# Convolution and pooling projections behind all gates, the weight split behind a step's events, and another form of the norm's scale

## The chip, the cores and the metric

The kernel runs on one core of a Trainium2 chip. The metric is the device time of one execution in microseconds. The kernel before took 1755.76 us, the median of three runs (1753.92 to 1758.45).

## The reference

The reference is one inference step of a two-layer network on 128 context tokens and 256 latent tokens, which share all weights. Each layer is a feed-forward block, a token mixer and another feed-forward block, each followed by a layer norm and modulated by a condition vector:

```
h = x * (1 + mod[3i+1]) + mod[3i]                         # modulate(i)
x = layer_norm(ALPHA*x + 0.5*mod[2]*swiglu(modulate(0)))
z = h @ w_in + b_in                                       # mixer, h = modulate(1)
q, k, v, cg, pu, gt = split(z)
att  = diff_attention(q, k, v) -> rms_norm -> @ w_att_o
conv = silu(layer_norm(depthwise_conv(a * sigmoid(g)))) @ w_conv_o     # 31 taps
pool = multiscale_pool(pu) @ w_pool_o
ga, gc, gp = split(sigmoid(gt))
x = layer_norm(ALPHA*x + mod[5] * ((ga*att + gc*conv + gp*pool) @ w_out + b_out))
x = layer_norm(ALPHA*x + 0.5*mod[8]*swiglu(modulate(2)))
```

All tensors are float32. The mod vectors are `silu(cond) @ w_mod`, 144 column blocks of 128, computed while the rest runs.

## The kernel before

All 384 tokens go through every matmul together, features on the partitions. A weight unit is a 128x1024 block of weights, and there is a fixed list of them (`_unit_specs`), in the order in which TensorE uses them. Each fp32 product is made of three fp32r matmuls (`mm3`, L402): the weights are split into a high part `wh`, cast by ScalarE (L342), and a low part `wl`, subtracted by VectorE (L351). So a unit is 24 matmuls of 384 columns. It has five buffer pairs (`NW`), and in some stretches (`extra`) up to four more, made of six of the 66 general slots of 128x384.

All instructions are written in an order fixed by hand. `begin(key)` (L372) opens a unit, a step: it prepares the units up to `lead` ahead (DMA, cast, split), then runs the events that are due at this step (`at(n, fn)`, `run_events`), then the folds (`run_after`), then `bg_rate` items of the background queue `bg`, then VectorE's modulation work, of which `mod_rate` jobs per unit are due. Each engine takes its instructions in that order. In the output projection of the mixer (`early`) the events run ahead of the preparation. `lead` starts at two behind a norm and rises by one per unit to five plus `extra`.

A mixer opens with units for the convolution's input (multiplied inside the norm), then q and k (steps 1 to 6), v (7 to 10), the pooling input (11, 12), the gates for attention and convolution (13 to 28). From step 13 the ten attention tasks run as events, one begun every second step: scores on TensorE, maximum on VectorE, exponentials on ScalarE, then transposition and product. `GP_ORDER` (L110) gives what follows: the eight pooling gates (`w_in` 0 to 7), and between pairs of them the four combined projections `cp`, each for two blocks of 128 features of the convolution and of the pooling. A projection takes four of the six PSUM banks tagged `mm`; a gate takes one. The evacuation of a projection (L1572 to L1574), an event of the next step, multiplies by the gates kept in slots. Then come four attention projections `ao`, four `w_out` units at once (`kouter`) and four more one by one.

The background queue holds 62 convolution taps (L1096), then the start of the convolution's chain (its seven events come 2 to 11 steps later), then 15 pooling items, of which the last starts the pooling matmuls one and two steps later. At the first `cp` whatever is left is drained. The root mean square of the attention output is scaled at L1512, transposed and split at L1517 to L1521.

A norm (`ln_end`, L674) overlaps the next stage: the first units of the next stage are multiplied with the unnormalized sum in eight folded parts, while the statistics (L543, one-column matmuls) go to VectorE, which computes mean and reciprocal root on 128x3 numbers; the two results are spread over the partitions with the identity (L745) into R and M.

Of the kernel before, what the change touches and what calls it, by code (L numbers as in the profile page):

```python
# [11 lines left out]
F32 = mybir.dt.float32  # L12
F32R = mybir.dt.float32r
BF16 = mybir.dt.bfloat16
I32 = mybir.dt.int32
# [4 lines left out]
D = 1024  # L20
# [77 lines left out]
BG = (4, 4, 3, 3, 2)  # L98
# [7 lines left out]
RATES = (0.9, 0, 0.65, 0.65, 0, 0.3)  # L106
# [3 lines left out]
GP_ORDER = [("w_in", 0), ("w_in", 1)]  # L110
for _mp in range(4):
    GP_ORDER.append(("cp", _mp))
    GP_ORDER += [("w_in", m) for m in (2 + 2 * _mp, 3 + 2 * _mp) if m < 8]

# [128 lines left out]
class Kernel:  # L243
# [5 lines left out]
    def __init__(self, tc, ctx, io):  # L249
# [4 lines left out]
        self.early = False  # L254
        self.half = None
# [41 lines left out]
    def tiny(self, n, dt=F32, name="y"):  # L297
        return self.pool.tile([128, 16], dt, name=self.nm(name), tag="tiny", bufs=24)[:, :n]
# [24 lines left out]
    def prep(self, upto):  # L323
        while self.n_prep < min(upto, len(UNITS)):
            self.prep_h()
            self.prep_l()

    def prep_h(self):
        u = self.n_prep
        slots = sum(not isinstance(w[0], SlotUnit) for w in self.w.values()) >= self.NW - self.held  # L330
        self.n_prep += 1
        self.dma_w(u + 1)
        cols = UNITS[u][1]
        r = self.raw.pop(u)
        if slots:
            w = tuple(SlotUnit([self.slot(F32R, n) for _ in range(3)]) for n in ("wh", "wl"))
        else:
            w = tuple(self.pool.tile([128, 1024], F32R, name=self.nm(n), tag=n, bufs=self.NW) for n in ("wh", "wl"))
        step = NT if slots else cols
        cuts = [slice(a, min(a + step, cols)) for a in range(0, cols, step)]  # L340
        for c in cuts:
            self.nc.scalar.copy(w[0][:, c], r[:, c])  # L342
        self.w[u] = w
        self.half = (u, r, cuts)

    def prep_l(self):
        u, r, cuts = self.half
        self.half = None
# [23 lines left out]
    def begin(self, key, run=True):  # L372
# [3 lines left out]
        if self.early:  # L376
            self.run_events()
        self.prep(u + self.lead)
        self.run_events()
        self.lead = min(self.lead + 1, self.NW + self.extra)  # L380
# [292 lines left out]

    def ln_end(self, b7, ab, keys):  # L674
# [51 lines left out]
        ms, msq, v = self.tiny(3), self.tiny(3), self.tiny(3)  # L726
        rm, rh, rl = self.tiny(6), self.tiny(6, F32R), self.tiny(6, F32R)
        nc.vector.tensor_scalar(ms, tot[:, 0:3], 1.0 / D, None, ALU.mult)
        nc.vector.tensor_tensor(msq, ms, ms, ALU.mult)
        nc.vector.scalar_tensor_tensor(v, tot[:, 3:6], 1.0 / D, msq, ALU.mult, ALU.subtract)  # L730
        self.rsqrt(v, 3, out=rm[:, 0:3])
        nc.vector.scalar_tensor_tensor(rm[:, 3:6], ms, -1.0, rm[:, 0:3], ALU.mult, ALU.mult)
        nc.vector.tensor_copy(rh, rm)
        nc.vector.tensor_sub(rl, rm, rh.bitcast(F32))
# [7 lines left out]
        for o, B in ((0, R), (3, M)):  # L742
            for t in range(3):
                for n, x in enumerate((rh, rl)):
                    mm(B[:, 128 * t:128 * t + 128], x[:, o + t:o + t + 1].to_broadcast([128, 128]),  # L745
                       self.identr, start=n == 0, stop=n == 1)
# [91 lines left out]
    def ffn(self, l, j, xs, outs, s, mod_rate):  # L838
# [26 lines left out]
        if fo:  # L865
            o2 = self.kouter([("ffn_in", l, j, 2), ("ffn_in", l, j, NF + 2)], xs, 8, KIN)
# [35 lines left out]
    def start(self):  # L902
# [10 lines left out]
        self.identr = self.t([128, 128], F32R, name="identr")  # L913
# [11 lines left out]
    def start_rest(self):  # L925
# [12 lines left out]
        self.at(4, lambda: nc.vector.tensor_copy(self.identr, self.ident))  # L938
# [96 lines left out]
    def mixer(self, l, xs, outs, s):  # L1035
# [575 lines left out]
        self.early = True  # L1611
# [23 lines left out]
    def build(self):  # L1635
# [3 lines left out]
        for s in range(6):  # L1639
# [7 lines left out]
            self.early = False  # L1647
# [47 lines left out]
```

## Time and profile before

| | us |
|---|---|
| median of three runs | 1755.76 |
| profiled execution | 1757.04 |
| its span, first to last instruction | 1755.3 |
| TensorE busy | 1706.0 |
| VectorE busy | 1303.9 |
| ScalarE busy | 769.1 |
| GpSimd busy | 305.4 |
| mean granted TensorE clock | 0.987 |

The span is what the profile sees of one execution; 1.7 us of the execution lie around it. A busy time is the union of an engine's instructions. TensorE's matmuls are pipelined: one of 384 columns is shown with 0.34 us, and the next starts about half of that later, so its busy time says where it stood, not how full it was. The feed-forward stage of the first layer runs up to 315 us, the first mixer to 600, two feed-forward stages to 1170, the second mixer to 1456, and the last feed-forward stage to 1737.

### The profile page before, as it was taken

The numbers are of one execution on the slowest core, as the hardware profiler recorded it, in microseconds if no ns is written. First come the engines' busy times: TensorE is split into PE (matmuls) and PEld (weight loads), VectorE is DVE, ScalarE is ACT, GpSimd is POOL, SyncE is SP. The second block draws the span as 40 slices with busy tenths as digits, with TensorE's granted clock in tenths as the row PEclk, the third lists the DMA queues.
The fourth block names the chain that finished last, engine by engine and source line by source line (L and its number), as shares of the span: only waits on it lengthen the run. The fifth ranks groups of instructions, "written<-read, shape, count | busy, mean of one in ns | idle before, by whom it ended". The sixth has DMA issues, their size and how long they took to land.

```text
span 1755.3 us, 26189 instructions
## 1 busy us (share of the span) xinstructions
PE 1706.0 (97%) x9734; PEld 1677.3 (96%) x9734; DVE 1303.9 (74%) x2268; ACT 769.1 (44%) x1377; POOL 305.4 (17%) x410
## 2 busy tenths in 40 slices
PE   7999999999999999999999999999899999999997
PEld 5999999998999999999999999999899999999997
DVE  3699997898868588878688787869996767753333
ACT  3523333755554383333364333347455436533332
POOL 0000023331313420001220000224222253000011
PEclk8999999999999999999999999999999999999998
DMA  9777766335434147666537666643444422654320
GB/s 364 255 230 227 234 219 210 121 106 161 136 110 143 60 143 231 213 199 207 185 109 217 206 209 195 217 132 119 140 126 115 145 76 84 196 162 117 121 75 36
DMA packets 86639, 287.45 MB, mean 164 GB/s; under 512 B 10096, under 2 KB 17520, under 8 KB 86512
## 3 DMA queue, kind: packets, MB, share of 16 engines
q1 hardware_dynamic: 86512, 285.79, 51.6%
q8 instruction: 76, 1.25, 0.3%
q14 instruction: 51, 0.42, 0.1%
HBM read 280.51 MB, written 2.62 MB: 161 GB/s over the span
## 4 chain that ended last, share of the span: by engine, by line
PE 79%; DVE 13%; ACT 4%; issue 3%; DMA 0%; SPq 0%; ACTq 0%; POOL 0%; DVEq 0%; POOLq 0%
PE mm L404 24%; PE mm L406 24%; PE mm L405 24%; DVE wl L351 4%; DVE acc L1096 2%; ACT wh L342 1%; PE mm L702 1%; PE mm L700 1%; PE mm L699 1%; PE mm L426 1%; PE mm L429 1%; PE mm L427 1%; PE tot L543 1%; PE m L959 0%; DVE hf L829 0%
## 5 line engine op out<-in xcount | busy, mean ns | idle before, releaser
L351 DVE TENSOR_TENSOR wl<-raw,wh 128x1024 fp32r<-128x1024 f32 (+3 forms) x438 | 480.3, 1113 | 319.9 <-ACT wh L342 308.7
L342 ACT CAST wh<-raw 128x1024 fp32r<-128x1024 f32 (+3 forms) x438 | 400.4, 934 | 613.5 <-issue 403.4
L404 PE MATMUL mm<-xh,wh 128*128 128x384 f32 x1796 | 611.8, 341 | 9.9 <-ACT e L1458 4.2
L405 PE MATMUL mm<-xh,wl 128*128 128x384 f32 x1796 | 608.5, 339 | 0.6 <-DVE wl L351 0.6
L406 PE MATMUL mm<-xl,wh 128*128 128x384 f32 x1796 | 608.5, 339 | 0.1
L404 PEld LDWEIGHTS mm<-xh,wh 128*128 128x128 f32 x1796 | 339.5, 189 | 15.4 <-ACT e L1458 4.6
L405 PEld LDWEIGHTS mm<-xh,wl 128*128 128x128 f32 x1796 | 339.6, 189 | 1.1 <-DVE wl L351 1.0
L406 PEld LDWEIGHTS mm<-xl,wh 128*128 128x128 f32 x1796 | 339.6, 189 | 0.4 <-DVE xl L833 0.4
L451 DVE SCALAR_TENSOR_TENSOR junk<-raw,scb 128x1024 bf16<-128x1024 f32 x256 | 312.4, 1220 | 4.5
L406 PE MATMUL mm<-al,wh 128*128 128x384 f32 x704 | 237.4, 337 | 0.0
L405 PE MATMUL mm<-ah,wl 128*128 128x384 f32 x704 | 237.3, 337 | 0.0
L404 PE MATMUL mm<-ah,wh 128*128 128x384 f32 x704 | 237.2, 337 | 0.0
L622 POOL TENSOR_SCALAR sq<-sq 128x384 f32<-128x384 f32 x6 | 7.0, 1173 | 784.9 <-ACT sq L619 784.9
L404 PEld LDWEIGHTS mm<-ah,wh 128*128 128x128 f32 x704 | 132.2, 188 | 0.0
L406 PEld LDWEIGHTS mm<-al,wh 128*128 128x128 f32 x704 | 132.2, 188 | 0.0
L405 PEld LDWEIGHTS mm<-ah,wl 128*128 128x128 f32 x704 | 132.2, 188 | 0.0
L1096 DVE SCALAR_TENSOR_TENSOR acc<-U,P,acc 128x399 f32<-128x399 f32 x120 | 85.7, 770 | 0.0
L619 ACT ACTIVATE sq<-X 128x384 f32<-128x384 f32 x42 | 22.1, 526 | 124.3 <-DVE X L608 123.3
L658 DVE SCALAR_TENSOR_TENSOR yl<-X,ab,yh 128x128 fp32r<-128x128 f32 x80 | 46.7, 608 | 24.9 <-ACT yh L656 24.6
L833 POOL TENSOR_TENSOR xl<-hf,xh 128x384 fp32r<-128x384 f32 x40 | 44.3, 1123 | 102.1 <-DVE t L771 83.6
L628 POOL TENSOR_TENSOR s<-s,X 128x384 f32<-128x384 f32 x30 | 30.6, 1019 | 170.2 <-DVE X L608 145.9
L853 ACT CAST ah<-a 128x384 fp32r<-128x384 f32 x88 | 44.3, 509 | 22.1 <-DVE a L849 22.1
(284 smaller groups left out, 2082.7 us busy)
## 6 DMA issues: line engine op xcount, KB each, us to landing
raw<-in_units SPq DMA_DIRECT2D x356, 512.0 KB, 3.8
raw<-in_wmod SPq DMA_DIRECT2D x144, 512.0 KB, 4.4
raw<-in_units SPq DMA_DIRECT2D x32, 384.0 KB, 3.7
X<-in_x SPq DMA_DIRECT2D x4, 384.0 KB, 7.1
K<-K SPq DMA_DIRECT2D x16, 96.0 KB, 5.0
out_y<-X SPq DMA_DIRECT2D x8, 192.0 KB, 2.0
scb<-in_cond SPq DMA_DIRECT2D x2, 512.0 KB, 8.2
Q<-QL SPq DMA_DIRECT2D x16, 64.0 KB, 4.7
```

The source lines that it names most:

```text
L342: self.nc.scalar.copy(w[0][:, c], r[:, c])
L351: self.nc.vector.tensor_sub(wl[:, c], r[:, c], wh[:, c].bitcast(F32))
L404: mm(out, wh, xh, start=first, stop=False)
L405: mm(out, wl, xh, start=False, stop=False)
L406: mm(out, wh, xl, start=False, stop=last)
L451: self.nc.vector.scalar_tensor_tensor(self.junk, r, 1.0, self.scb[:, c, :], ALU.mult, ALU.mult, accum_out=mv[:, j, c:c + 1])
L619: nc.scalar.activation(sq, x, AF.Square)
L628: nc.gpsimd.tensor_add(st["s1"], st["s1"], x)
L658: nc.vector.scalar_tensor_tensor(lo[:, a:b], x[:, a:b], self.ab[:, 0, m, c:c + 1], h[:, a:b].bitcast(F32), ALU.mult, ALU.subtract)
L833: (nc.gpsimd if pool else nc.vector).tensor_sub(xl, hf, xh.bitcast(F32))
L853: nc.scalar.copy(h, a)
L1096: nc.vector.scalar_tensor_tensor(acc[c][:, :399], U[c][:, j:j + 399], w, acc[c][:, :399], ALU.mult, ALU.add)
```

## The change

The projections `cp` come behind all eight pooling gates. The background queue gives three items per unit throughout the mixer instead of four in the first ten units. In `begin` the casts of the weights are still issued first, but the splits on VectorE come behind the step's events, unless `lead` is below four; the `early` case goes. The norm's mean and reciprocal root are computed in 15 instructions with two refinements (the second of higher order) instead of 18 with three, without the bias of the variance by 1/D, and the results are spread by fp32 matmuls with the fp32 identity instead of a pair of fp32r matmuls. The modulation rate of the two middle feed-forward stages is 0.7 instead of 0.65, and each stage behind a norm starts two units' worth of modulation below zero. There are 32 tiny buffers instead of 24. The core of the diff:

```diff
-BG = (4, 4, 3, 3, 2)
+BG = (3, 3, 3, 3, 2)
...
-RATES = (0.9, 0, 0.65, 0.65, 0, 0.3)
+RATES = (0.9, 0, 0.7, 0.7, 0, 0.3)
...
-GP_ORDER = [("w_in", 0), ("w_in", 1)]
-for _mp in range(4):
-    GP_ORDER.append(("cp", _mp))
-    GP_ORDER += [("w_in", m) for m in (2 + 2 * _mp, 3 + 2 * _mp) if m < 8]
+GP_ORDER = [("w_in", m) for m in range(8)] + [("cp", m) for m in range(4)]
...
-        self.early = False
-        self.half = None
+        self.half = []
...
-        return self.pool.tile([128, 16], dt, name=self.nm(name), tag="tiny", bufs=24)[:, :n]
+        return self.pool.tile([128, 16], dt, name=self.nm(name), tag="tiny", bufs=32)[:, :n]
...
     def prep(self, upto):
+        self.prep_cast(upto)
+        self.prep_sub()
+
+    def prep_cast(self, upto):
         while self.n_prep < min(upto, len(UNITS)):
             self.prep_h()
+
+    def prep_sub(self):
+        while self.half:
             self.prep_l()
...
-        self.half = (u, r, cuts)
+        self.half.append((u, r, cuts))
...
-        u, r, cuts = self.half
-        self.half = None
+        u, r, cuts = self.half.pop(0)
...
         self.step += 1
-        if self.early:
-            self.run_events()
-        self.prep(u + self.lead)
+        self.prep_cast(u + self.lead)
+        if self.lead < 4:
+            self.prep_sub()
         self.run_events()
+        self.prep_sub()
         self.lead = min(self.lead + 1, self.NW + self.extra)
...
+    def ln_scale(self, tot):
+        nc = self.nc
+        S, Q = tot[:, 0:3], tot[:, 3:6]
+        rm = self.tiny(6)
+        t = lambda dt=F32: self.tiny(3, dt, "rs")
+        nm, s2, v, i, h = t(), t(), t(), t(I32), t()
+        nc.vector.tensor_scalar(nm, S, -1.0 / D, None, ALU.mult)
+        nc.vector.tensor_tensor(s2, S, nm, ALU.mult)
+        nc.vector.tensor_tensor(v, Q, s2, ALU.add)
+        nc.vector.tensor_scalar(i, v.bitcast(I32), -0.5, float(0x5F3759DF), ALU.mult, ALU.add)
+        nc.vector.tensor_scalar(h, v, -0.5, None, ALU.mult)
+        y0 = i.bitcast(F32)
+        a, b, y, yd = t(), t(), t(), t()
+        nc.vector.tensor_tensor(a, y0, y0, ALU.mult)
+        nc.vector.tensor_tensor(b, a, h, ALU.mult)
+        nc.vector.scalar_tensor_tensor(y, b, 1.5, y0, ALU.add, ALU.mult)
+        a, b, u, w = t(), t(), t(), t()
+        nc.vector.tensor_tensor(a, y, y, ALU.mult)
+        nc.vector.tensor_scalar(yd, y, math.sqrt(D), None, ALU.mult)
+        nc.vector.scalar_tensor_tensor(b, a, -1.0, v, ALU.mult, ALU.mult)
+        c = math.sqrt(0.375)
+        nc.vector.tensor_scalar(u, b, 1.0, c, ALU.add, ALU.mult)
+        nc.vector.scalar_tensor_tensor(w, u, 0.5 / c, u, ALU.add, ALU.mult)
+        nc.vector.scalar_tensor_tensor(rm[:, 0:3], w, 1.0, yd, ALU.add, ALU.mult)
+        nc.vector.tensor_tensor(rm[:, 3:6], nm, rm[:, 0:3], ALU.mult)
+        return rm
...
-        ms, msq, v = self.tiny(3), self.tiny(3), self.tiny(3)
-        rm, rh, rl = self.tiny(6), self.tiny(6, F32R), self.tiny(6, F32R)
-        nc.vector.tensor_scalar(ms, tot[:, 0:3], 1.0 / D, None, ALU.mult)
-        nc.vector.tensor_tensor(msq, ms, ms, ALU.mult)
-        nc.vector.scalar_tensor_tensor(v, tot[:, 3:6], 1.0 / D, msq, ALU.mult, ALU.subtract)
-        self.rsqrt(v, 3, out=rm[:, 0:3])
-        nc.vector.scalar_tensor_tensor(rm[:, 3:6], ms, -1.0, rm[:, 0:3], ALU.mult, ALU.mult)
-        nc.vector.tensor_copy(rh, rm)
-        nc.vector.tensor_sub(rl, rm, rh.bitcast(F32))
+        rm = self.ln_scale(tot)
...
-        for o, B in ((0, R), (3, M)):
-            for t in range(3):
-                for n, x in enumerate((rh, rl)):
-                    mm(B[:, 128 * t:128 * t + 128], x[:, o + t:o + t + 1].to_broadcast([128, 128]),
-                       self.identr, start=n == 0, stop=n == 1)
+        self.bcast(R, rm[:, 0:3])
+        self.bcast(M, rm[:, 3:6])
...
+        if fo:
+            self.mod_acc = -2 * mod_rate
...
-        self.at(4, lambda: nc.vector.tensor_copy(self.identr, self.ident))
...
-        self.early = True
...
-            self.early = False
```

## Rows read from the trace of the kernel before

**Rows 1.** Page, section 1: busy us, share and instructions of each engine.

```profile
PE 1706.0 (97%) x9734; PEld 1677.3 (96%) x9734; DVE 1303.9 (74%) x2268; ACT 769.1 (44%) x1377; POOL 305.4 (17%) x410
```

**Rows 2.** What TensorE (PE) waited for: us in total, times, longest us.

```profile
PE sm L745 <- DVE y L733: 6.5, 4, 3.5
PE sm L1483 <- ACT wT L1477: 5.3, 4, 2.0
PE mm L404 <- ACT e L1458: 4.2, 2, 2.1
PE mm L426 <- DVE t L1593: 3.0, 2, 1.5
PE mm L700 <- DVE wl L351: 2.4, 2, 1.2
PE sm L405 <- DVE wpl L1329: 2.2, 2, 1.1
PE mm L404 <- ACT PB L1260: 1.8, 2, 0.9
PE mm L406 <- DVE ol L1521: 1.4, 2, 0.7
```

**Rows 3.** By stretch: us; PE, PEld, DVE, ACT, POOL busy; granted clock; DMA; GB/s.

```profile
404.10:407.50 3.40, 3.40 (x13) 3.40 (x12) 2.36 (x6) 2.29 (x3) 0.00 (x0) 0.50 0.65 179
469.00:472.40 3.40, 3.40 (x11) 3.40 (x12) 3.33 (x7) 1.45 (x3) 2.83 (x8) 0.50 0.67 165
1322.30:1329.10 6.80, 6.50 (x19) 5.88 (x20) 6.39 (x12) 2.85 (x6) 5.88 (x11) 0.50 0.56 155
602.10:608.90 6.80, 6.80 (x26) 6.80 (x26) 5.83 (x27) 2.76 (x7) 0.00 (x0) 0.50 0.28 87
```

**Rows 4.** VectorE's groups by shape: busy us, mean ns; idle before, releaser.

```profile
L351 DVE TENSOR_TENSOR wl<-raw,wh 128x1024 fp32r<-128x1024 f32 x331 | 412.4, 1252 | 287.3 <-ACT wh L342 281.4
```

**Rows 5.** ScalarE in time: start, us, engine line op [idle before <-releaser].

```profile
402.54 0.37 ACT L1458 ACTIVATE e<-mm,y 128x128 f32<-128x128 f32 x1 [9.07 <-DVE y L1454]
```

**Rows 6.** VectorE in order of time, first norm's chain, four of 17.

```profile
315.66 0.16 DVE L728 TENSOR_SCALAR y<-tot 128x3 f32<-128x3 f32 x1 [1.03 <-PE tot L543]
316.45 0.17 DVE L516 TENSOR_SCALAR rsi<-rsi 128x3 int32<-128x3 int32 x1
316.65 0.16 DVE L522 TENSOR_TENSOR rsa<-rsi 128x3 f32<-128x3 f32 x1
318.61 0.17 DVE L733 CAST y<-y 128x6 fp32r<-128x6 f32 x1
```

**Rows 7.** TensorE's groups: the broadcasts of spread and of the conv means.

```profile
L536 PE MATMUL sm<-C,y 128*128 128x128 f32 x18 | 2.5, 274 | 0.0
```

**Rows 8.** VectorE in order of time, first mixer: four taps, twice.

```profile
355.88 3.78 DVE L1096 SCALAR_TENSOR_TENSOR acc<-U,P,acc 128x399 f32<-128x399 f32 x4
381.93 2.26 DVE L1096 SCALAR_TENSOR_TENSOR acc<-U,P,acc 128x399 f32<-128x399 f32 x4
```

**Rows 9.** Busy time by stretch (columns as in rows 3): the same taps.

```profile
355.90:359.50 3.60, 3.60 (x22) 3.60 (x22) 3.60 (x5) 3.46 (x7) 3.17 (x4) 1.00 0.45 175
381.95:384.10 2.15, 2.15 (x14) 2.15 (x13) 2.15 (x5) 1.93 (x2) 0.00 (x0) 1.00 0.50 91
```

**Rows 10.** ScalarE in order of time, last projection of the first mixer.

```profile
596.27 0.53 ACT L619 ACTIVATE sq<-X 128x384 f32<-128x384 f32 x1 [2.43 <-DVE X L608]
596.70 1.03 ACT L342 CAST wh<-raw 128x1024 fp32r<-128x1024 f32 x1
```

**Rows 11.** VectorE in order of time: a projection's evacuation; the scaling.

```profile
505.86 0.55 DVE L1572 SCALAR_TENSOR_TENSOR pm<-ga,mm 128x384 f32<-128x384 f32 x1
536.50 2.43 DVE L1512 TENSOR_SCALAR o<-o,rsy 128x128 f32<-128x128 f32 x12
```

**Rows 12.** ScalarE in order of time: the casts of two units in one step.

```profile
520.85 2.18 ACT L342 CAST wh<-raw 128x1024 fp32r<-128x1024 f32 x4 [3.26 <-issue]
```

**Rows 13.** Busy time by stretch (columns as in rows 3): first feed-forward stage.

```profile
60.00:300.00 240.00, 240.00 (x1377) 240.00 (x1376) 215.55 (x348) 83.71 (x127) 19.43 (x23) 1.00 0.70 225
```

More of the change, by code (lines that the diff above doesn't have):

```diff
@@ L912, in start @@
         self.ones = self.t([128, 1], name="ones")
-        self.identr = self.t([128, 128], F32R, name="identr")
         self.ident = self.C[:, C_ID:C_ID + 128]
```

## The prediction

> **What bounds the kernel now.** I read the page's busy shares first. TensorE is busy for 1706.0 of 1755.3 us, VectorE for 1303.9 [rows 1]. So nothing but TensorE's 49.3 us of idle time, and its time at half clock, can be won; work taken from another engine is worth nothing by itself. Next, the table of what TensorE waited for [rows 2]. The eight groups shown hold 26.8 us; of the other 22.5 I count nothing. The first, 6.5 us, is the four norms in which TensorE runs dry while VectorE works through the variance (three by about 1 us, the last by 3.5). The other seven, 20.3 us, come in pairs or fours because the two mixers each have them: the exponentials of the prompt's attention (4.2), the transposed weights (5.3), the pooling matmuls (2.2), the bank that w_out needs (3.0), the low weights at the mixer's norm (2.4), the pooling evacuation (1.8), the low part of the attention output (1.4). Third, the granted clock by stretch [rows 3]: four stretches, 20.4 us, ran at 0.50. TensorE's two levels are 1.2 and 2.4 GHz, so these cost about 10.2 us. Ahead of the first three stood one of those mixer waits, ahead of the fourth the wait for low weights and then the one-column statistics matmuls.
>
> Then, who is late. VectorE's largest idle group is the weight split: 281.4 us behind ScalarE's cast [rows 4]. In begin() the split is issued ahead of the step's events, so when the cast is late, every reduction and evacuation of the step stands behind it on VectorE; the cast is late when ScalarE waits for VectorE. The proof is one line: ScalarE stood 9.07 us for VectorE's maximum of the first prompt task [rows 5], and TensorE then waited for those exponentials.
>
> **The change part by part.** The sums are made against the profiled execution, 1757.04 us (span 1755.3 plus 1.7 around it); the median of the three runs, 1755.8, is 1.3 lower and the forecast is stated against that.
>
> *Short norm chain.* Before, 17 VectorE instructions lead from the first statistic to the operand of the first broadcast; first and last start 2.95 us apart [rows 6]. The two intervals around an instruction that doesn't depend on the one ahead (L518, between 316.45 and 316.65) are 0.20 together; the 14 others are 2.75 / 14 = 0.196. After, R's operand is the 14th instruction, and two of the 13 ahead (`h`, `yd`) are independent: 9 x 0.196 + 2 x 0.20 = 2.16, so 0.8 saved; bounds 0.5 (all 13 at the mean of 0.184) and 1.0. It counts where TensorE runs dry: four norms, 3.2 us. At the mixers' two norms other matmuls cover the chain: 0. The broadcasts go from 12 fp32r matmuls per norm to six in fp32; fp32 makes two records of each matmul (18 for the nine of `spread` and the two conv means) [rows 7], so 12 records stay 12: 0. At 2.5 / 18 = 0.14 us a record 12 take 1.7 us; the bounds are half of that either way, 0.8. The dropped copy of the identity and eight more tiny buffers: 0.
>
> *Split after the events.* ScalarE's order hardly changes (casts still lead); on VectorE the events go first. In the gates a wait of up to 1.03 us for a cast [rows 10] plus a split of 1.25 [rows 4] no longer stands before each reduction. The wait that this adds is the split's, behind events that themselves wait; queued behind it on VectorE are the folds, the taps and the modulation, and its reader is TensorE three or more units on. I take 0; C below prices it if that cover is gone.
>
> *Three steps a unit instead of four.* From step 2 to step 10 nine taps fewer per mixer run. The taps take 0.95 us each beside GpSimd (four in 3.78 us while GpSimd was busy 3.17 of 3.60) or 0.57 (four in 2.26, GpSimd 0.00) [rows 8, 9]: nine are 5.1 to 8.5 us less VectorE work ahead of the values' evacuation and the first maximum; I take 6, and the split behind it adds 1.2. Of the 9.07 us of lateness about 7 go, and TensorE stood only 2.1 us of it in each mixer, so the exponentials' 4.2 us go wholly. By counting the queue (15, 12 and 6 taps, then three a gate) the taps end ten gates in, the conv chain is done at step 33, the pooling at 29; the first projection is now step 37. So no drain of the queue is paid at it: 0; had it not been done, each conv step would stand bare.
>
> The seven waits then: exponentials 4.2 of 4.2; transposed weights 5.0 of 5.3; pooling 2.0 of 2.2, as `low` now leads its step; w_out's bank 2.8 of 3.0, since the evacuation of ao no longer stands behind a split; low weights at the norm 2.0 of 2.4; pooling evacuation 1.0 of 1.8 (there the cast still leads); attention output 0. Sum 17.0 us, bounds 10 and 20.3. For the norm: with `early` gone the last cast (596.70) no longer stands behind the evacuation and the square (596.27) [rows 10]; it can start when its buffer comes free, an evacuation of 0.55 [rows 11] and the square's 0.43 sooner, about 1 us of the 1.2 that each norm waits. What is late next there: the square, then GpSimd's sums; both have the two leading matmul groups as cover.
>
> *Half clock.* If the waits go, the first three stretches, 13.6 us, go with them: 6.8 us. Of the fourth's 3.4 us I take half, 1.7, as the statistics matmuls stay; bounds 3 and 10.2 together.
>
> *Projections behind the gates.* Each takes four of the six banks, so the second half of each needs banks that the previous one's four evacuations (0.55 us each) free. Next to them now stand scale (12 instructions, 2.43 us) [rows 11], and on ScalarE, from the fourth projection on, the casts of two units in a step (2.18 us) [rows 12], because `extra` is set at the second one; the transposes' evacuation waits behind these casts. Walking VectorE's queue: the second half of the third projection is some 0.5 us late (bias, scale and one evacuation, of which all but 2.6 run ahead, against the 12 matmuls of its first half, 2.1). That of the fourth is 1.6 late: casts 2.2, two evacuations of the transposes and one of a projection with the steps between, 2.2, against 2.1 and six transposes, 0.7 (12 records at 0.06, an estimate from the half of a broadcast's). The attention output is 0.6 later than now, by a second unit's cast. That is 2.7 per mixer, 5.4 in all; bounds 0 (VectorE ran ahead) and 15. The gates' results stay longer, up to 24 slots, but the 16 of xs come free before the extra units want theirs: 0. SP's queue carries the same units, one transfer each, nine ahead, in the new order, and GpSimd the same two sums per projection: 0.
>
> *Modulation at 0.7, two units later.* The number of jobs (128) is unchanged; in the feed-forward stages TensorE is busy throughout with VectorE at 215.55 of 240 us even at rate 0.9 [rows 13]: 0. The cover left there is 24.4 us in 57 units (1377 matmuls, 24 to a unit), 0.43 a unit; the two more jobs per later stage, 2.5 us each, find more.
>
> **Sum.** 3.2 + 17.0 + 6.8 + 1.7 - 5.4 = 23.3 us. 1757.0 - 23.3 = 1733.7 for a run like the profiled one; against the median, 1732.
>
> **Rivals.** *A, VectorE's load is the limit, not its order.* The taps only move: nine a mixer go to steps 20 to 22, where GpSimd builds a stack and a tap costs 0.38 more [rows 8, 9], and the pooling steps now meet the modulation. Then the pooling waits stay (2.0), half of the transposed weights (2.5) and of the exponentials (2.1), and two half-clock stretches (5.1): 11.7 dearer, 1744. For it: in both stretches with taps VectorE was busy to the full [rows 9]. Against: the 281 us of waiting for casts are rest that the new order can use. The Trainium skill, "GPSIMD Engine Reference", section 1, has GpSimd share its SBUF interfaces with VectorE, in contention with VectorE instructions of two SBUF inputs; the taps are such, and the trace agrees (0.95 against 0.57 us). By that rule the nine moved taps would cost up to 3.4 us of VectorE per mixer, a part of this rival's reason and no term of its sum.
>
> *B, the bank wait is larger.* If each of three following projections waits for all four evacuations, 2.2 us, that is 6.6 instead of 2.7 per mixer, and a half-clock stretch of 3.4 (1.7) follows: 5.6 x 2 = 11.2 dearer, 1743. Against: no wait for L1572 stands among TensorE's today [rows 2], and two banks are always left.
>
> *C, slower.* With the split last, VectorE now waits in its events for ScalarE's results behind the cast and only then splits. If one cast, 1.03 us, is exposed in each of the 53 units of the first feed-forward stage with modulation, 0.60 over the spare 0.43 falls on TensorE: 32 us, 1764. It decides from 0.43 us a unit, and is slower than now only above 0.87. Against: casts start at the unit's head, and the lead is three units or more wherever the split goes last.
>
> *D, it does not do what it says.* The waits are ScalarE's order (cast first), which stays: only the chain's 3.2 us is won, 1753.
>
> **How the numbers follow.** Forecast 0.62, A 0.16, B 0.10, C 0.06, D 0.06. A measurement here tells about 0.3%, 5.3 us, from no change. Faster: forecast, A and B, 0.88; same: D, 0.06; slower: C, 0.06. Low end: all of the seven waits, the chain, all 10.2 of the clock and no new wait, 33.7, make 1722, and 4 more for smaller waits at the same places: 1718. High end: A and B together with 0.7 of their prices, 16, 1748.
>
> **What would show it.** After, TensorE's waits for the prompt's exponentials, for the transposed weights and for the w_out bank should be gone, the wait for the norm's operand about 0.2 us in three norms and 2.7 in the last; new waits for the evacuations L1572 and for `ol` near the third and fourth projections. Half clock should be found at most near the mixers' norms. Waits for low weights in the feed-forward stages would make C right; the same 20 us of mixer waits in other lines would make A right.

## The result and the profile after

The changed kernel takes 1728.74 us, the median of four runs (1727.91 to 1730.71), against 1755.99 for the kernel before in the same comparison: a ratio of 0.9846, with a 95% interval of 0.9829 to 0.9863. That is 27.2 us less, where 23.3 were forecast; the time lies 3.3 us below the forecast of 1732. The profiled execution has a span of 1726.2 us, 29.1 less than that of before. The 27.2 are the difference that counts; the traces' 29.1 serve to say where it lies.

The page's busy times after, against [rows 1]: TensorE lost 13.5 us of busy time, while VectorE and GpSimd have more. TensorE is now idle for 33.7 us instead of 49.3.

```profile
PE 1692.5 (98%) x9734; PEld 1665.3 (96%) x9734; DVE 1321.2 (77%) x2241; ACT 769.5 (45%) x1369; POOL 342.9 (20%) x410
```

What TensorE waited for after (us in total, times, longest), against [rows 2]. The start's waits for data are left out; they are alike in both.

```profile
PE mm L429 <- DVE t L1614: 3.5, 2, 1.8
PE sm L539 <- DVE y L702: 3.3, 4, 2.7
PE mm L407 <- DVE pm L1593: 3.3, 2, 1.6
...
PE mm L407 <- ACT oh L1541: 2.1, 2, 1.0
PE sm L1504 <- ACT wT L1498: 1.9, 2, 1.0
```

Gone are the exponentials, the pooling matmuls, the low weights at the norm, the pooling evacuation and the low part `ol`. The norm's wait is 3.3 instead of 6.5. The transposed weights of the prompt are at 1.9 instead of 5.3. The wait for w_out's banks (L429, L426 before) is still there, and has grown from 3.0 to 3.5. Two waits are new: for a projection's evacuation (L1593, L1572 before) and for the high part of the attention output, `oh`. Two more small waits of before, that the prediction did not count, are gone too:

```profile
PE sm L404 <- DVE y L1133: 1.3, 2, 0.6
PE sm L404 <- ACT wT L1424: 0.8, 2, 0.5
```

The granted clock (seventh value behind the stretch's length; columns as in rows 3). Of the four stretches of [rows 3], and a fifth of before that I had passed over (first fence, at 1458.80), one is left between the start and the last norm (second fence).

```profile
1458.80:1462.20 3.40, 3.40 (x12) 3.40 (x13) 2.98 (x16) 1.67 (x5) 0.00 (x0) 0.50 0.45 123
```

```profile
590.70:594.10 3.40, 3.40 (x13) 3.40 (x13) 2.72 (x18) 0.63 (x2) 0.00 (x0) 0.50 0.52 149
```

Who is late is read from the weight split on VectorE (the group by shape: busy us, mean ns, then the idle time before it). Before, VectorE idled 287.3 us ahead of it [rows 4]; now it is 89.9. Most of the rest stands ahead of the products of the feed-forward stages, which now come first and which TensorE nowhere waits for.

```profile
L353 DVE TENSOR_TENSOR wl<-raw,wh 128x1024 fp32r<-128x1024 f32 x335 | 421.0, 1262 | 89.9 <-ACT wh L345 89.7
...
L875 DVE TENSOR_TENSOR al<-a,ah 128x384 fp32r<-128x384 f32 x88 | 48.6, 557 | 80.2 <-ACT ah L874 76.6
L870 DVE TENSOR_TENSOR a<-mm,si 128x384 f32<-128x384 f32 x82 | 45.5, 556 | 75.9 <-ACT si L868 71.0 <-PE mm L409 3.0
```

The norms serve as marks in time: the start of TensorE's first broadcast of the variance's result, where TensorE runs dry. The rows are those of the first and last norm after (start, us, instruction, wait before it); the table has all four, read in the same way.

```profile
316.60 0.38 PE L539 MATMUL sm<-C,y 128*128 128x128 f32 x1 [0.20 <-DVE y L702]
...
1714.04 0.55 PE L539 MATMUL sm<-C,y 128*128 128x128 f32 x1 [2.72 <-DVE y L702]
```

| norm | starts before, us (wait) | starts after, us (wait) |
|---|---|---|
| first | 318.84 (1.00) | 316.60 (0.20) |
| third | 891.81 (0.99) | 876.64 (0.20) |
| fourth | 1173.58 (1.00) | 1157.72 (0.19) |
| last | 1743.08 (3.51) | 1714.04 (2.72) |

From one mark to the next the gain is 2.2 us up to the first, 12.9 from the first to the third (first mixer, and the feed-forward stage behind it), 0.7 from the third to the fourth, and 13.2 from the fourth to the last (second mixer and the last stage): 29.0 in all, and 26.1 of it where the mixers are.

### The profile page after: what moved, and what is told of

Same layout as the page of the kernel before. It is cut to its first block, busy times and chain, and to the rows that moved or that the text cites. A ratio compares the mean times of both kernels' runs of the same rounds, so it can differ in the third digit from the quotient of the medians.

```text
span 1726.2 us, 26047 instructions
## 1 busy us (share of the span) xinstructions
PE 1692.5 (98%) x9734; PEld 1665.3 (96%) x9734; DVE 1321.2 (77%) x2241; ACT 769.5 (45%) x1369; POOL 342.9 (20%) x410
## 4 chain that ended last, share of the span: by engine, by line
PE 90%; DVE 6%; ACT 2%; issue 1%; DMA 0%; SPq 0%; POOL 0%; ACTq 0%; DVEq 0%; POOLq 0%
PE mm L407 26%; PE mm L408 26%; PE mm L409 26%; DVE wl L353 3%; PE mm L731 1%; PE mm L732 1%; PE mm L734 1%; PE mm L429 1%; PE mm L432 1%; PE mm L430 1%; DVE acc L1117 1%; ACT wh L345 1%; PE m L980 1%; PE sm L539 1%; PE tot L546 1%
## 5 line engine op out<-in xcount | busy, mean ns | idle before, releaser
L353 DVE TENSOR_TENSOR wl<-raw,wh 128x1024 fp32r<-128x1024 f32 (+3 forms) x430 | 489.8, 1154 | 112.4 <-ACT wh L345 112.2
L875 DVE TENSOR_TENSOR al<-a,ah 128x384 fp32r<-128x384 f32 x88 | 48.6, 557 | 80.2 <-ACT ah L874 76.6
L870 DVE TENSOR_TENSOR a<-mm,si 128x384 f32<-128x384 f32 x82 | 45.5, 556 | 75.9 <-ACT si L868 71.0
L631 POOL TENSOR_TENSOR s<-s,X 128x384 f32<-128x384 f32 x30 | 39.6, 1320 | 148.9 <-DVE X L611 126.2
L661 DVE SCALAR_TENSOR_TENSOR yl<-X,ab,yh 128x128 fp32r<-128x128 f32 x80 | 58.7, 770 | 6.2 <-ACT yh L659 6.0
```

What stands on the lines that cost most here:

```text
L353: self.nc.vector.tensor_sub(wl[:, c], r[:, c], wh[:, c].bitcast(F32))
L631: nc.gpsimd.tensor_add(st["s1"], st["s1"], x)
L661: nc.vector.scalar_tensor_tensor(lo[:, a:b], x[:, a:b], self.ab[:, 0, m, c:c + 1], h[:, a:b].bitcast(F32), ALU.mult, ALU.subtract)
L870: nc.vector.tensor_mul(a, u[:, :NT], sl)
L875: nc.vector.tensor_sub(lo, a, h.bitcast(F32))
```

## The experiments

Times are medians of four runs or more. The ratios are to the kernel before, run on the same chip.

| kernel | us | ratio, 95% interval |
|---|---|---|
| after | 1728.7 | 0.9846 [0.9829, 0.9863] |
| 1, before with the new split order alone | 1734.0 | 0.9872 [0.9859, 0.9886] |
| 2, before with the new norm chain alone | 1755.0 | 0.9994 [0.9985, 1.0003] |
| 3, after with the projections between the gates | 1727.1 | 0.9835 [0.9821, 0.9848] |
| 4, after with the old split order | 1772.1 | 1.0090 [1.0076, 1.0104] |
| 5, after, extra units 2 steps earlier | 1728.9 | 0.9842 [0.9827, 0.9857] |
| 6, after, no extra units in the mixers | 1732.0 | 0.9860 [0.9845, 0.9874] |
| 7, after with four steps a unit | 1740.6 | 0.9907 [0.9890, 0.9923] |
| 8, after with the old modulation rates | 1731.5 | 0.9856 [0.9841, 0.9870] |
| 9, after, extra units 4 steps earlier | 1724.5 | 0.9824 [0.9809, 0.9839] |
| 10, after, extra units 5 steps earlier | 1721.2 | 0.9803 [0.9789, 0.9818] |
| 11, after with the old norm chain | 1732.2 | 0.9869 [0.9853, 0.9886] |
| 12, as 10, first prompt product a step later | 1724.8 | 0.9816 [0.9802, 0.9829] |

The theory: the time came from VectorE's order, events ahead of the split, and from the half clock that followed the waits. The rival: it came from VectorE's load, the taps at three a unit.

### 1. The split order alone

The new `prep_cast`, `prep_sub` and `begin` in the kernel before:

```diff
-        if self.early:
-            self.run_events()
-        self.prep(u + self.lead)
+        self.prep_cast(u + self.lead)
+        if self.lead < 4:
+            self.prep_sub()
         self.run_events()
+        self.prep_sub()
```

> The kernel before, with one part of the change alone: a step's weight splits on VectorE come behind the step's events (and the case of the output projection goes). Taps at four, projections between the gates, the long norm chain and the old modulation rates stay. My theory, order: most of the seven mixer waits (17.0 us in the prediction) came of the split standing ahead of the events. The part that I gave to the nine moved taps, about half of the exponentials' 4.2, stays; the rest, some 15 us of waits, and three half-clock stretches, 6.8, go: 1734 us (1730 to 1740). Rival A, load: the taps decide, the order does little; only the bank wait and the pooling wait go, 5 us: 1751. Rival C: a split that comes too late shows as waits of TensorE for low weights in the feed-forward stages; the time would be 1756 or more.

Measured 1734.0, 22.0 us less, the number that the theory gave. Rivals A and C fall; of C's waits for low weights in the feed-forward stages one is there, of 0.84 us (634.83, behind the first mixer's norm; before has none). But the way is not wholly the expected one. The exponentials do not keep half of their wait; they have none. In their place stands a new wait of 7.0, in which TensorE holds the second half of the first prompt task:

```profile
PE mm L1454 <- POOL QL L1381: 7.0, 2, 3.5
```

The row names GpSimd, but look at VectorE in order of time: the values' evacuation (L1248), which frees the bank that this matmul writes, starts at 391.15 behind four taps a step, and the matmul at 392.04.

```profile
388.37 2.27 DVE L1102 SCALAR_TENSOR_TENSOR acc<-U,P,acc 128x399 f32<-128x399 f32 x4
...
391.15 0.74 DVE L1248 TENSOR_TENSOR vp<-mm,bv 128x256 f32<-128x256 f32 x2
```

That the number is met to the microsecond is partly luck. By the rows the waits are 12.6 us shorter (21.6 gone; new or longer are this 7.0, 0.7 at a mixer's norm, 0.5 for transposed weights and the 0.84), where some 15 were expected, and 13.6 us of half clock are left of 23.8 (392.00, 1235.10 and 1436.50), 5.1 us where 6.8 were expected. That is 17.7 of the 23.3 us between the two spans.

### 7. Four background steps a unit

```diff
-BG = (3, 3, 3, 3, 2)
+BG = (4, 4, 3, 3, 2)
```

> The kernel after, with four background steps a unit in the first ten units again. My theory: the split order alone leaves TensorE waiting 3.5 us per mixer for the banks of the values, whose evacuation stands behind four taps a step, with a half-clock stretch behind it; three a step removed that. With four, these 7.0 us and about 3.4 us of half clock come back: 1739 (1735 to 1741). Rival: with the projections behind the gates the taps are idle filling; four a step end the taps and the pooling earlier and cost nothing: 1727 to 1730.

Measured 1740.6, 11.8 more than after, and the wait of experiment 1 is back, with two half-clock stretches behind it (394.60 and 1237.60):

```profile
PE mm L1469 <- POOL QL L1396: 6.9, 2, 3.5
```

The same evacuation on VectorE, in after (first fence) and here (second):

```profile
385.88 0.74 DVE L1263 TENSOR_TENSOR vp<-mm,bv 128x256 f32<-128x256 f32 x2
```

```profile
392.41 0.74 DVE L1263 TENSOR_TENSOR vp<-mm,bv 128x256 f32<-128x256 f32 x2
```

So once the split order is new, three taps a unit are needed for the values' banks. The rival, that they are filling, falls.

### 3. The projections between the gates

```diff
-GP_ORDER = [("w_in", m) for m in range(8)] + [("cp", m) for m in range(4)]
+GP_ORDER = [("w_in", 0), ("w_in", 1)]
+for _mp in range(4):
+    GP_ORDER.append(("cp", _mp))
+    GP_ORDER += [("w_in", m) for m in (2 + 2 * _mp, 3 + 2 * _mp) if m < 8]
```

> The kernel after, with the eight pooling gates and the four projections in the old order (two gates, a projection, two gates, and so on). My theory: the projections behind the gates cost 5.4 us, so this kernel takes 1723.5 (1720 to 1727), and the waits for the projections' evacuations and for the high part of the attention output are gone. Rival: the late projections are what gives the three-a-unit background queue its room. The first projection would then be step 31, while the convolution's chain, started by the last tap at step 22, has its last event 11 steps later; two or more of its steps and the last pooling steps are drained in front of the first projection with TensorE idle, 2 to 5 us per mixer and a half-clock stretch with each: 1733 to 1742.

Measured 1727.1, just past the upper end of the theory's range; its interval overlaps that of after. Both mechanisms are in the trace, and in the time they nearly cancel. The waits for L1593, `oh` and w_out's banks, 8.9 us in after, are gone. In their place TensorE waits 7.8 us in front of the first projection (first fence). There the rest of the convolution's chain is drained: the step's events run ahead of time, ScalarE is still at the exponentials and the convolution's activations (second fence, ScalarE), and the copy of the transposed weights that TensorE wants is last.

```profile
PE sm L1454 <- ACT wT L1448: 7.8, 2, 3.9
```

```profile
486.49 0.57 ACT L1431 ACTIVATE e<-mm,y 128x384 f32<-128x384 f32 x1
...
487.05 0.70 ACT L1168 ACTIVATE cz<-cd,P 128x384 f32<-128x384 f32 x1
...
488.21 0.56 ACT L1562 ACTIVATE ga<-mm,bh 128x384 f32<-128x384 f32 x1
488.67 0.47 ACT L1448 COPY wT<-sm 128x384 f32<-128x384 f32 x1
```

The half clock that the rival forecast stands behind these waits, 6.8 us in the first mixer (below) and 3.4 in the second (1331.50), where after has 3.4 in all:

```profile
488.40:495.20 6.80, 6.00 (x21) 6.01 (x22) 3.95 (x11) 2.39 (x7) 0.00 (x0) 0.50 0.18 69
```

By these rows the kernel should be some 2 us slower than after (8.9 of waits saved; paid are 7.8 of waits, and 3.4 for 6.8 us more of half clock). Why it is not stays open.

### 4. The old split order in the kernel after

The reverse of the diff of experiment 1, in the kernel after.

> The kernel after, with the old order of the weight split (cast and split ahead of the step's events, the events first only in the output projection of the mixer). Three background steps a unit, the projections behind the gates, the new norm chain and modulation rates stay. My theory, order: the mixer waits that the old order makes come back, all but half of the exponentials': some 12 to 15 us, with two or three half-clock stretches, 5 to 7: 1747 (1742 to 1752). Rival A, load: three steps a unit did most of it, and the kernel stays within 5 us of after: 1729 to 1734.

Measured 1772.1: 43.3 more than after, 16.1 more than before. Both expectations fall, but on the side of the order. The rest of the change without the new order is a loss. Half of it is half clock, 40.8 us between the start and the last norm against 23.8 before (8.5 us); the waits grow mostly at the projections. Their banks are Rival B of the prediction, at 13.8 us about the size that it had (6.6 per mixer):

```profile
PE mm L401 <- DVE pm L1587: 13.8, 6, 3.6
...
PE mm L423 <- DVE t L1608: 4.7, 2, 2.4
```

VectorE in order of time shows it: it stands 2.17 us for the cast, splits, adds the bias and scales, and only then evacuates the projection that TensorE waits for (until 538.40, 3.57 us).

```profile
533.85 1.23 DVE L348 TENSOR_TENSOR wl<-raw,wh 128x1024 fp32r<-128x1024 f32 x1 [2.17 <-ACT wh L339]
534.99 0.54 DVE L565 TENSOR_SCALAR X<-X,gc 128x128 f32<-128x128 f32 x2
535.45 2.43 DVE L1527 TENSOR_SCALAR o<-o,rsy 128x128 f32<-128x128 f32 x12
537.80 0.54 DVE L1587 SCALAR_TENSOR_TENSOR pm<-ga,mm 128x384 f32<-128x384 f32 x1
```

Not all waits of before came back with the old order: none for the prompt's exponentials or the pooling evacuation, and 0.3 us of the 2.2 for pooling. So these go with the new order alone (experiment 1), and without it too, where the taps and the projections are as in after.

### 2 and 11. The norm chain

`ln_scale` and `bcast` in the kernel before; and, in 11, the old chain in the kernel after. The core of both, one way or the other:

```diff
-        self.rsqrt(v, 3, out=rm[:, 0:3])
...
+        rm = self.ln_scale(tot)
...
+        self.bcast(R, rm[:, 0:3])
+        self.bcast(M, rm[:, 3:6])
```

> The kernel before, with the norm's new chain alone: 15 small VectorE instructions with two refinements, and fp32 broadcasts with the fp32 identity. My theory: four norms in which TensorE runs dry are shorter by 0.8 us each, and the broadcasts cost what they did: 3.2 us, 1752.6, and TensorE's wait for the first broadcast's operand is about 0.2 us three times and 2.7 us once instead of 1.0 and 3.5. Rival: the broadcasts in fp32 take more than the pairs did, by up to 0.8 us a norm, and all is given back: 1756.

> The kernel after, with the norm's old chain and its pair of fp32r broadcasts. My theory: TensorE's wait for the broadcasts' operand is 6.5 us again instead of 3.3, and the time 1732 (1731 to 1733). Rival, as the chain alone on the kernel before suggests: part of the 3.2 us is given back elsewhere in the norm; the kernel takes 1729 to 1730.

The waits go as forecast, 3.3 (four times, longest 2.7) in kernel 2 and 6.5 in kernel 11, one row each:

```profile
PE sm L536 <- DVE y L699: 3.3, 4, 2.7
```

```profile
PE sm L748 <- DVE y L736: 6.5, 4, 3.5
```

The times say 1.1 us with an interval from 2.6 less to 0.5 more on the kernel before, and 3.5 on the kernel after, where the runs of the two kernels (1727.9 to 1730.7, 1731.8 to 1733.5) do not overlap (by the ratios it is 4.0). 2.6 us is short of 3.2; four other waits in kernel 2's trace are longer by 1.0 together, none by more than 0.4. That part stays open; on the kernel that matters the term holds.

### 8. The modulation rates

```diff
-RATES = (0.9, 0, 0.7, 0.7, 0, 0.3)
+RATES = (0.9, 0, 0.65, 0.65, 0, 0.3)
...
-        if fo:
-            self.mod_acc = -2 * mod_rate
```

> The kernel after, with the old modulation rates (0.65 in the two middle feed-forward stages) and without the start two units below zero. My theory: TensorE is busy throughout the feed-forward stages at either rate, so nothing changes: 1727 to 1730. Rival: without the start below zero the first modulation jobs, 2.5 us of VectorE each, stand ahead of the evacuations right behind a norm, where lead is two or three units; TensorE then waits for low weights there, 0.5 to 1 us in each of three norms: 1730 to 1732.

Measured 1731.5, in the rival's range; the interval overlaps that of after. The trace has one wait that after has not, 40 us behind the first mixer's norm, of 0.72 us:

```profile
635.53 0.44 PE L408 MATMUL mm<-xh,wl 128*128 128x384 f32 x1 [0.72 <-DVE wl L353]
```

Before has no such wait. Experiment 1, with the new order and the old rates, has it in the same place:

```profile
634.83 0.44 PE L411 MATMUL mm<-xh,wl 128*128 128x384 f32 x1 [0.84 <-DVE wl L356]
```

So it is the new split order that makes this wait, and the new rates that take it away: beside the order they are worth at least that much, against the kernel before nothing. The rest of the 2.8 us (1.8 by the ratios) can't be told from no change.

### 5, 6, 9 and 10. The extra units

After experiment 3 the question was what makes the three waits of 8.9 us. VectorE in order of time after, in the attention projections, against a step of some 4 us:

```profile
537.18 3.49 DVE L353 TENSOR_TENSOR wl<-raw,wh 128x1024 fp32r<-128x1024 f32 x4
...
542.47 4.15 DVE L353 TENSOR_TENSOR wl<-raw,wh 128x1024 fp32r<-128x1024 f32 x4
546.54 1.00 DVE L1614 SCALAR_TENSOR_TENSOR t<-ga,mm 128x384 f32<-128x384 f32 x2
547.47 1.01 DVE L1619 TENSOR_TENSOR t<-t,pm 128x384 f32<-128x384 f32 x2
548.41 4.12 DVE L353 TENSOR_TENSOR wl<-raw,wh 128x1024 fp32r<-128x1024 f32 x4
552.45 1.01 DVE L1614 SCALAR_TENSOR_TENSOR t<-ga,mm 128x384 f32<-128x384 f32 x2
```

Two units a step are split there, because `extra` lets `lead` rise; with 2.0 us of evacuation each step takes 6, and w_out's matmul waits for the evacuation of 552.45 until 553.05. The other two waits are ScalarE's two-unit casts: the attention output's `oh` stands behind one, and so does the evacuation that the fourth projection waits for until 529.17. VectorE stands for `oh` ahead of it, and the first two-unit split (530.43) comes only behind it:

```profile
527.51 1.14 DVE L1542 SCALAR_TENSOR_TENSOR ol<-sm,gsub,oh 128x384 fp32r<-128x384 f32 x2 [1.29 <-ACT oh L1541]
528.58 0.54 DVE L1593 SCALAR_TENSOR_TENSOR pm<-ga,mm 128x384 f32<-128x384 f32 x1
```

The experiments move the steps at which `extra` rises (2, then 4) in the kernel after. In 5 it rises after the sixth and the eighth pooling gate, in 9 after the fourth and the sixth, in 10 after the third and the fifth; in 6 it stays at 0 (`EXTRA = 0`). The edit of 10:

```diff
             if kind == "w_in":
                 gate(34 + mp, tcp, (1, mp))
+                if mp == 2:
+                    self.extra = EXTRA // 2
+                if mp == 4:
+                    self.extra = EXTRA
                 continue
...
-            if mp == 1:
-                self.extra = EXTRA // 2
...
-        self.extra = EXTRA
```

> The kernel after, with the four extra weight units granted earlier: two after the sixth pooling gate and two after the last, instead of two at the second projection and two at the first attention projection. The steps in which two units are cast and split are then the last gate and the first three projections, and no longer the fourth projection and the first three attention projections. My theory now: in after, the two-unit splits (3.5 to 4.15 us of VectorE in steps of 4 us) and the two-unit casts (2.18 us of ScalarE ahead of the attention output's high part) make the three new waits of TensorE, 8.9 us in two mixers: for the evacuation of the third projection (3.3), for the high part of the attention output (2.1) and for the banks of w_out (3.5). With them gone or below 0.3 each: 1720 to 1722. Rival: the waits come of the projections' four banks each and of the attention sums themselves, whatever is split beside them; they stay or move one projection ahead, and the time stays within 2 us of after: 1727 to 1730.

> The kernel after, with no extra weight units in the mixers: never more than five units are prepared there, and no step of the projections casts or splits two. My theory: the three waits of 8.9 us go as in the kernel with the units granted earlier; but the four units that w_out's second half and the norm lived on must now be cast and split beside the norm's evacuations, so waits for low weights come back there (2.4 us in the kernel before, and a half-clock stretch of 3.4 us in each): 1723 to 1728. Rival, that splits beside the projections don't matter: the waits of 8.9 us stay and the norm's come on top: 1731 to 1734.

> The kernel after, with the extra units granted two steps earlier still: two after the fourth pooling gate and two after the sixth, so that the steps that cast and split two units are the sixth to eighth gate and the first projection. My theory now: a projection step of 4 us holds the evacuation of eight half products, 2.1 us of VectorE, and one split, and nothing more; the two-unit splits of 3.4 us there are what TensorE waits for, wherever in the projections they stand. A gate step leaves VectorE some 3 us idle. With the splits in the gates, only the first projection has a double one: its evacuations start late by 2 us at the second, and the waits of 5.8 us in the kernel with the units granted two steps later shrink to 1 to 2; those for the attention output and w_out's banks stay gone: 1721 to 1724. Rival: the projections' evacuations are late in themselves; the wait at the third stays 2.3 us per mixer: 1727 to 1729.

> As the kernel before this one, granted one gate earlier: all four steps that cast and split two units are gates, the fifth to the eighth, and the projections and the attention output cast and split one unit each. My theory: the wait for the projections' evacuations is what the kernel without extra units had there, 1.0 us in both mixers, and none stands at the attention output, at w_out's banks or at the norm: 1720 to 1722, the fastest. Rival: the general slots are held by the gates' results and by the modulated input until the last gate has run; the extra units then wait for slots on ScalarE, with the gates' evacuations queued behind: the waits move to the gates, 1726 to 1731.

Measured 1728.9, 1732.0, 1724.5 and 1721.2. The waits of TensorE near the projections in 5, 6, 9 and 10, in that order:

```profile
PE mm L407 <- DVE pm L1595: 5.8, 3, 2.2
```

```profile
PE mm L408 <- DVE wl L353: 4.7, 3, 2.1
PE tot L546 <- POOL s L631: 3.5, 2, 1.8
...
PE mm L407 <- DVE pm L1593: 1.0, 2, 0.5
```

```profile
PE mm L407 <- DVE pm L1595: 2.0, 4, 0.8
```

```profile
PE mm L407 <- DVE pm L1595: 1.0, 2, 0.5
```

In all four the waits for `oh` and for w_out's banks are gone: the two-unit steps made them. Experiment 5 came out at its rival's number: its two-unit splits stood in the first three projections, and the wait for evacuations grew from 3.3 to 5.8 as it moved there. It is not the projections' four banks as such: 6, without any such split, and 10, with all of them in the gates, have 1.0. 6 has its rival's number, but not its mechanism: the three waits fell to 1.0, and what was saved is spent behind, where w_out and the norm wait for low weights and for GpSimd's sums (8.2 us, 0.6 of them the start's) and half clock has grown from 3.4 us to 13.6 (590.00 and 1433.10). 9 comes out half a microsecond above its theory's range, with the expected wait (2.0). Kernel 10 has neither of 6's waits, and at 1721.2 us it is 34.6 faster than before (by its ratio) and the fastest of all; its runs (1718.5 to 1723.0) lie below all of after's. Its rival, slots held by the gates, falls.

### 12. The first prompt task's product a step later

In kernel 10 the wait for the transposed weights, 1.9 us, is the largest left in the mixers.

```diff
-                self.at(n0 + sp * i + n, fn)
+                self.at(n0 + sp * i + n + (i == 0 and fn is d), fn)
```

> The kernel with all extra units granted in the gates, and the first prompt task's product one step later. In after, and in all kernels like it, TensorE waits about 1.0 us per mixer for that product's transposed weights, whose copy stands on ScalarE behind the exponentials of the second prompt task. My theory: the step between gives it cover, the wait of 1.9 us in two mixers goes, and nothing else waits for the product: 1719.3 (1718 to 1721). Rival: the step that now holds two transposes and two products has both small banks taken, and the wait moves to the second task: within 1 us of the kernel without this edit, 1720.5 to 1722.

Measured 1724.8, 3.6 more than 10 by the medians, which come from two chips, and 2.3 by the ratios to before, whose intervals overlap. The theory falls, and the rival's mechanism is not the one seen either. The first task no longer waits; the second waits 2.0 us in each mixer, with a half-clock stretch behind it in each (422.60 and 1258.80). ScalarE in order of time: the first task's product is now read (L1509 and L1511, two of each, the first row one of them) ahead of the copy `wT` for the second, which was in time before.

```profile
419.46 0.38 ACT L1509 ACTIVATE o<-sm,y 128x128 f32<-128x128 f32 x1
...
420.66 0.41 ACT L1498 COPY wT<-sm 128x256 f32<-128x256 f32 x1
```

## Why the prediction was right, and where it was not

**The direction and the main cause held.** The split order alone brings 22.0 of the 27.2 us (experiment 1), and without it the rest loses (experiment 4). Rival A falls by experiment 1, though for some of the waits VectorE's load would have done as well (experiment 4). C falls by the absence of waits for low weights in the feed-forward stages (from the third norm to the fourth the time fell by 0.7 us, about the chain's 0.8), and D with the waits.

**The step that failed is w_out's bank.** The prediction took 2.8 of its 3.0 us, "since the evacuation of ao no longer stands behind a split". It doesn't within its own step, but the splits of the step ahead still stand before it, and there are two units of them; I had counted ScalarE's two-unit casts (2.18 us) and not VectorE's two-unit splits of 3.5 to 4.15. In its place stand 3.5 us, as the rows under experiments 5 to 10 show.

**Terms that were mis-sized.** The transposed weights gave 3.4 instead of 5.0, the low weights at the norm 2.4 instead of 2.0, the pooling evacuation 1.8 instead of 1.0, the attention output 1.4 instead of 0, pooling 2.2 instead of 2.0. With the bank's +0.5 for -2.8, the seven waits fall by 14.9, where 17.0 were forecast; two small waits that I had not counted add 2.1. The half clock gave more: before, I had counted four stretches and there was a fifth; 23.8 us became 3.4 between the start and the last norm, worth 10.2 us instead of 8.5. The split order's own price was set at 0 for the feed-forward stages; it is one wait of 0.7 to 0.8 us, and the modulation's new rates, also set at 0, take it back (experiments 1 and 8).

**Terms that held.** The chain: waits shorter by 3.2. The projections behind the gates: 5.4 was the sum of 0.5, 1.6 and 0.6 per mixer; measured are 0, 1.6 and 1.0, together 5.4 (3.3 for L1593 and 2.1 for `oh`). Its reason held: the two-unit casts stand ahead of both waits, and with the two-unit steps moved away all but 1.0 goes. What it left out is the two-unit splits, which make w_out's wait.

**The sum by rows**: 3.2 + 14.9 + 2.1 + 10.2 - 5.4 = 25.0 of the 29.1 us between the two spans. Of the other 4.1, 1.4 lie ahead of the first norm (2.2 less the chain's 0.8), in the start, where before ran 3.4 us at half clock (25.20 to 28.60) that after has not; 2.7 in the mixers I can't place.

**What I had not seen is that the parts need each other.** The taps' share of the exponentials was not what the taps are needed for: the order alone frees these too (experiment 1), and with it the three a unit are needed for the values' banks (7.0, experiments 1 and 7). Three a unit end the convolution later, so that projections between the gates pay a drain of 7.8 (experiment 3), to which the prediction had given a sentence and no price. Moving them behind the gates takes that away and costs 8.9, of which all but about 1 is the place of the extra units (experiment 10). So the taps and the projections, taken together, add little to the order. By experiments 1, 11 and 8, the kernel with the new order, chain and rates and the old taps and projections would take 1734.0 - 3.5 - 2.8 = 1727.7 to 1734.0 - 3.5 = 1730.5 us, an estimate; after takes 1728.7. By that estimate they pay once the extra units are moved (1721.2); no run has moved the extra units without them.

## What to carry to other kernels

On an in-order engine, put what someone waits for ahead of what only runs ahead for later units, and then check every step in which the run-ahead does double work: its backlog falls on the evacuations of the next steps. Count such a step on each engine, split as well as cast, against the time that TensorE takes for it. When several moves lean on each other, price each with the others undone too; here the taps and the projections together are worth next to nothing as placed, by the estimate above, and yet 11.8 us is lost when the taps alone are taken back (experiment 7).

## What the runs showed of the hardware

The same split of two units (four instructions) took 2.52 us of VectorE in a gate of experiment 5 (first fence), but in after 3.49 us beside GpSimd's sums of the projections (2.26 of 3.40 us) and 4.15 beside its split of the gated sum (3.11 of 4.10; second fence, columns as in rows 3). In the gate GpSimd was busy too, 1.57 of 2.40 us, but with instructions on 12 columns:

```profile
510.57 2.52 DVE L353 TENSOR_TENSOR wl<-raw,wh 128x1024 fp32r<-128x1024 f32 x4 [2.89 <-ACT wh L345]
```

```profile
537.20:540.60 3.40, 3.40 (x21) 3.40 (x20) 3.40 (x5) 2.19 (x4) 2.26 (x2) 1.00 0.36 77
542.50:546.60 4.10, 4.10 (x26) 4.10 (x25) 4.10 (x6) 2.68 (x6) 3.11 (x2) 1.00 0.73 236
```

By the Trainium skill, "GPSIMD Engine Reference", section 1, GpSimd shares its SBUF interfaces with VectorE, in contention with VectorE instructions of two SBUF inputs. The split has two such inputs, and these rows agree: up to 1.63 us more for the same work. The difference between 2.52 and 4.15 us lies in two of the four instructions, of 384 columns (0.55 and 0.57 us against 1.37 and 1.38); the one of 1024 columns took 1.22 to 1.23 in both. The other side pays as well: GpSimd in order of time, beside the split of the first fence, the same operation on 12 columns ahead of the split and beside it:

```profile
509.55 0.24 POOL L531 TENSOR_SCALAR rsa<-rsa 128x12 f32<-128x12 f32 x1
...
510.75 1.14 POOL L531 TENSOR_SCALAR rsa<-rsa 128x12 f32<-128x12 f32 x1
```

It took 0.24 us alone and 1.14 beside the split. On VectorE this is a part of why the two-unit steps cost what they did.

Half clock did not need a wait. Ahead of the stretch at 590.70 TensorE waited for nothing; from 588.34 on it ran the norm's 24 statistics matmuls of one column, the first and the last six of which are:

```profile
588.34 0.72 PE L546 MATMUL tot<-ones,s 128*128 128x1 f32 x6
...
590.27 1.08 PE L546 MATMUL tot<-ones,sq 128*128 128x1 f32 x6
```

In kernel 10, too, the only such stretches between the start and the last norm stand behind these matmuls (587.00 and 1423.30). They don't always bring it: the same matmuls at the second mixer's norm of after (from 1429.48 on) ran at a granted clock of 1.00, and so did what followed. That they alone make the clock fall was not tried.
